# Running the whole gated embedding before the experts, and adding it to the stream in SBUF

## The chip, the cores and the metric

The kernel runs on one core of a Trainium2 chip. The metric is the device time of one execution in microseconds (us); lower is better. Three executions before the change gave a median of 1067.1 us.

## The reference, cut to what matters

The model has two layers (DEPTH = 2) on a stream h of 512 tokens by 1024 columns. Behind the mixers and the first layer norm, each layer adds a mixture of 16 experts and a gated per-layer embedding, both computed from the same h, and normalises the sum:

```python
    h = layer_norm(DN_ALPHA * h + mix, ln1_g[i], ln1_b[i])
    y_moe = hier_moe(h, moe_wgc[i], moe_bgc[i], moe_wgf[i], moe_bgf[i],
                     moe_w1[i], moe_w3[i], moe_w2[i])
    y_ple = jax.nn.sigmoid(h @ ple_wg[i] + ple_bg[i]) * (p[i] @ ple_wp[i])
    h = layer_norm(DN_ALPHA * h + y_moe + y_ple, ln2_g[i], ln2_b[i])
```

An expert is a gated MLP of width 256 on the tokens routed to it: silu(t @ w1) * (t @ w3), then @ w2, weighted by its gate. Each token goes to 2 of the 16. The embedding's product h @ ple_wg is 512 x 1024 x 1024.

## The kernel before, in words

**Products.** Weights and activations are float32. A chunk of weights is loaded raw, split into a high and a low part (`split`, lines 224 and 225: ScalarE casts the high part, VectorE subtracts to get the low one), and each product is three matmuls (`mm3`, lines 218 to 220).

**The planner.** `plan` lists all units of weight work of a layer in order; a unit is one chunk, mostly 512 KB. `pump` issues a unit's loads on SP's queue (line 240) `ahead_raw` units ahead of the one that TensorE works on, and its split `ahead_split` units ahead. `fill(n)` emits n units, `fill_us(us)` emits pieces of units worth so many planned us (a piece of an embedding unit is one of its four token tiles, 6 matmuls), `fill_to` all up to a mark. Engines run in order, each in its own queue; the compiler may move independent instructions past one another.

**Slots.** Raw chunks, high and low parts, the stream tiles `h`, transposed tokens `xT`, expert outputs `ye`, and the embedding's `pwp`, `bg` and `plz` all take one of 33 slots of 4 KB a partition (`NSLOT`). A slot is given again only when its last user is done, be it a matmul or a store. Half-size tiles have 6 slots of their own.

**The embedding before.** `add_pwp` computes p @ ple_wp for both column halves ahead of it. `add_ple(i, c)` is the gate's product for half c: four units of 24 matmuls, with the four token tiles in four PSUM banks. At the last unit `ple_tile` adds the bias (VectorE), takes tanh (ScalarE) and multiplies by `pwp` (VectorE); every two token tiles, a DMA of POOL's queue adds the result to the DRAM array `yd` (`accum_op=OP.add`, line 1228). `norm1` has stored h both to `hd`, from which the experts gather, and to `yd`. Half 0 runs between routing and the experts. Half 1 is cut in two parts (`PLE_AT = 3, 12`): two units after expert 3, whose sums are kept in `plz`, and two after expert 12.

**The experts.** `layer` routes the tokens (`route`), gathers the rows of two experts from `hd` by indirect DMAs, tests whether any expert has over 128 tokens (`overflow`: every engine loads the count into a register and branches, lines 1343 and 1344), then loops over 16 experts. An expert has four units for w1 and w3 (24 matmuls) and two for w2 (12 matmuls), the latter emitted while the next expert's are under way. Its gathered rows are transposed first (`expert_x`, line 376), its activations in between (`expert_act`, line 1292). The outputs of 14 experts are added to `yd` by a scattering DMA (`scatter`, line 1257); the last two are added on TensorE after the stream has been read back from `yd` (`load_stream`, line 1411; `tail_sum`, line 1430).

**Loads ahead.** `P_MOE = 14, 3` holds from routing to expert 10, `P_END = 7, 3` from there (`E_END`), `P_LAST = 8, 4` at the last expert.

Of the kernel before, what the change touches and what calls it, by code (L numbers as in the profile page):

```python
# [13 lines left out]
AF = mybir.ActivationFunctionType  # L14
OP = mybir.AluOpType
# [136 lines left out]
class Trunk:  # L152
# [14 lines left out]
    ]  # L167
    N = [[5.5, 2.0, 1.5, 2], [5.5, 0, 3.5, 3.5]]
    R = [[3.0, 9.0], [6.0, 7.0]]
    W6 = [[2, 4, 1.5], [2, 2, 0.5]]  # L170
    E_END = 10
    PLE_AT = 3, 12
    P_LAST = 8, 4
    P_END = 7, 3
    P_LN = 14, 1
    P_MOE = 14, 3
    APART = [[], [0, 1, 3]]
    ZPE = [[1], [1, 2, 3]]

# [821 lines left out]
    def norm1(self, i, t):  # L1001

        self.ln_tile(t, t in self.APART[0])
        h = self.h[t]
        for dst in (self.hd, self.yd):
            self.nc.gpsimd.dma_start(dst[t * 128:(t + 1) * 128], h)
        self.dump(f"h1_{i}_{t}", h)


# [190 lines left out]

        self.add([(lambda r: r, self.A["ple_wp"][i][:, cs].rearrange("(k p) n -> p k n", p=128))], [2, 512], emit)

    def ple_tile(self, t, c, z, bias, o):

        nc = self.nc
        nc.vector.tensor_add(o, z, bias)
        nc.scalar.activation(o, o, AF.Tanh, scale=0.5)
        nc.vector.scalar_tensor_tensor(o, o, 1.0, self.pwp[c][t // 2][:, t % 2], op0=OP.add, op1=OP.mult)

    def add_ple(self, i, c, part=None):  # L1210

        nc = self.nc
        cs = slice(c * 512, (c + 1) * 512)
        qs = range(4) if part is None else range(part * 2, part * 2 + 2)
        st = {}

        def evac(t, ps):
            if part == 0:
                if t % 2 == 0:
                    self.plz[t // 2] = self.s4([128, 2, 512], "plz")  # L1220
                nc.vector.tensor_add(self.plz[t // 2][:, t % 2], ps, self.bg[:, cs])
            else:
                if part is None and t % 2 == 0:
                    self.plz[t // 2] = self.s4([128, 2, 512], "plz")
                z = self.plz[t // 2]
                self.ple_tile(t, c, ps, z[:, t % 2] if part else self.bg[:, cs], z[:, t % 2])
                if t % 2:
                    nc.gpsimd.dma_start(self.yd[(t - 1) * 128:(t + 1) * 128, cs].rearrange("(t p) n -> p t n", p=128),
                                        z, accum_op=OP.add)

        def emit(q):
            def f(wp):
                if q == qs[0]:
                    st["ps"] = [self.ps("pl") for _ in range(NT)]
                for t in range(NT):
                    for k in range(2):
                        self.mm3(st["ps"][t], [x[:, q * 2 + k, t * 128:(t + 1) * 128] for x in self.hT],
                                 [x[:, k] for x in wp], q == qs[0] and k == 0, q == qs[-1] and k == 1)
                    if q == qs[-1]:
                        evac(t, st["ps"][t])  # L1240
                    yield 1.28
            return f

        for q in qs:
            src = self.A["ple_wg"][i][q * 256:(q + 1) * 256, cs].rearrange("(k p) n -> p k n", p=128)
            self.add([(lambda r: r, src)], [2, 512], emit(q))

# [207 lines left out]
    def plan(self, i):  # L1455

        m = self.marks = getattr(self, "marks", {})
        here = lambda name: m.__setitem__((i, name), len(self.units))
        self.add_head(i, 0, before=lambda t: self.start_norm(i, t))
        self.add_hyena(i, 2)  # L1460
        self.add_hyena(i, 1)
        self.add_hyena(i, 0)
        self.add_pool(i)
        here("pool")
        self.add_head(i, 1)
        here("head1")
        self.add_mix(i, (0, 1, 6, 7), 0, True)
        self.add_head(i, 2)
        here("head2")
        self.add_mix(i, (0, 1, 6, 7), 1, True)  # L1470
        self.add_head(i, 3)
        here("head3")
        for c in range(2):
            self.add_mix(i, (2, 3, 4), c, False)
        here("mix")
        self.add_last_mix(i)
        here("last")
        self.add_pwp(i, 0)
        self.add_pwp(i, 1)
        here("pwp")  # L1480
        self.add_ple(i, 0)
        here("ple")
        for e in range(NE):

            self.add_expert_in(i, e)
            if e > 0:
                self.add_expert_out(i, e - 1)
            if e in self.PLE_AT:
                self.add_ple(i, 1, self.PLE_AT.index(e))
        self.add_expert_out(i, NE - 1)  # L1490
        here("end")

# [16 lines left out]
    def layer(self, i):  # L1509
        nc, A = self.nc, self.A  # L1510
# [94 lines left out]
        next(r)  # L1605
        self.fill_us(self.R[i][0])
        for _ in r:
            pass
        self.xe, self.xT, self.act, self.actT, self.yl, self.hotT, self.plz = {}, {}, {}, {}, {}, {}, {}
        self.ahead_raw, self.ahead_split = self.P_MOE  # L1610
        for e in range(2):
            self.xe[e] = self.gather(self.rows[:, e:e + 1])
        self.fill_us(self.R[i][1])
        self.overflow(i)
        self.fill_to(i, "ple")
        self.expert_x(0)
        for e in range(NE):
            self.fill(2)
            if e + 2 < NE:
                self.xe[e + 2] = self.gather(self.rows[:, e + 2:e + 3])  # L1620
            if e == self.E_END:
                self.gb = self.gain(A["ln2_g"][i], A["ln2_b"][i])
                self.ahead_raw, self.ahead_split = self.P_END
            if e + 1 < NE:
                self.expert_x(e + 1)
            self.fill(2)
            if e == NE - 1:
                self.load_stream()
            if e >= NE - NL:
                self.last_places(e)  # L1630
            if e == NE - 1:
                self.ahead_raw, self.ahead_split = self.P_LAST

                self.cap = self.marks[i, "end"] + 3
            if e > 0:
                self.fill(2)
            self.expert_act(e)
            if e in self.PLE_AT:
                self.fill(2)
        self.fill(2)  # L1640

    def build(self):
# [56 lines left out]
```

## Time and profile before

| what | value |
|---|---|
| median of 3 runs (lowest, highest) | 1067.1 us (1065.82, 1071.48) |
| the profiled execution: its own time | 1060.65 us |
| its span, first to last instruction | 1058.7 us |
| mean granted TensorE clock | 0.974 of full speed |
| TensorE busy | 977.4 us, 92% |
| VectorE, ScalarE, POOL busy | 74%, 58%, 16% |
| SP's DMA queue (weights) | 155.58 MB, 44.8% of the 16 DMA engines' span |
| POOL's DMA queue (gathers, scatters, stores, tables) | 40.87 MB, 15.1% |

The profile is of one execution; its sums are set against 1060.65 us, of which the span is all but 1.95 us. Times within it are counted from the span's start. In layer 0 the embedding's half 0 runs from 307 to 336 us and the experts from 339 to 539 us; in layer 1 from 810 to 838 us and from 842 to 1034 us.

### The profile page before, as it was taken

Reading aid. Unit: us, or ns where it says so; the run is one execution under the profiler, and the core shown is the slowest. Engines: PE = TensorE matmul, PEld = TensorE weight load, DVE = VectorE, ACT = ScalarE, POOL = GpSimd, SP = SyncE. Lnnn points to the kernel's source line nnn. Section 1 sums busy time; section 2 is a strip of 40 time slices with the busy share of each in tenths; the row PEclk is TensorE's granted clock in tenths of the full one; section 3 lists DMA queues with packets and bytes.
Section 4 is the critical chain, followed back from the end, with each engine's and each line's share of the span. In section 5 each row is a group of like instructions: output and inputs, shape, how many; then the busy total and the mean of one; then the engine's idle time right before and its main releaser. Section 6 shows DMA issues by size and latency. Waiting matters only on the chain. (4 is left out here: it accounts for less than half of the span.)

```text
span 1058.7 us, 14409 instructions
## 1 busy us (share of the span) xinstructions
PE 977.4 (92%) x4869; PEld 805.7 (76%) x4870; DVE 779.3 (74%) x1301; ACT 613.5 (58%) x1046; POOL 166.3 (16%) x170
## 2 busy tenths in 40 slices
PE   4999999999889898999999999999998989999895
PEld 3887889897767676777768889798776768877673
DVE  7576887767685676878885578847678677888776
ACT  5425464656552746887754246654645375887673
POOL 1101000000122112332121100000002222333112
PEclk9999999999999998999989999999999999999998
DMA  8815121231864988999994412122186498899974
GB/s 261 234 35 140 51 79 42 70 95 65 308 209 109 334 245 274 292 300 308 264 312 122 112 55 66 49 64 88 50 307 221 107 329 275 283 311 318 306 211 159
DMA packets 156010, 197.49 MB, mean 187 GB/s; under 512 B 20296, under 2 KB 123786, under 8 KB 155925
## 3 DMA queue, kind: packets, MB, share of 16 engines
q1 hardware_dynamic: 135253, 155.58, 44.8%
q0 software_dynamic: 20672, 40.87, 15.1%
q8 instruction: 42, 0.69, 0.3%
q14 instruction: 43, 0.35, 0.1%
HBM read 182.85 MB, written 29.36 MB: 200 GB/s over the span
## 5 line engine op out<-in xcount | busy, mean ns | idle before, releaser
L225 DVE TENSOR_TENSOR wlo<-raw,whi 128x1024 fp32r<-128x1024 f32 (+2 forms) x278 | 321.9, 1182 | 78.9 <-ACT whi L224 68.1
L224 ACT CAST whi<-raw 128x1024 fp32r<-128x1024 f32 (+2 forms) x278 | 275.0, 1025 | 42.1 <-DMA yd<-ye,rt_tok 11.0
L218 PE MATMUL e<-whi,xT 128*128 128x512 f32 x256 | 108.8, 425 | 3.5 <-ACT xT L224 1.8
L219 PE MATMUL e<-wlo,xT 128*128 128x512 f32 x256 | 106.0, 414 | 5.9 <-DVE wlo L225 5.9
L220 PE MATMUL e<-whi,xT 128*128 128x512 f32 x256 | 103.4, 404 | 0.0
L218 PE MATMUL pj<-whi,hT 128*128 128x384 f32 x256 | 89.8, 351 | 2.3 <-ACT hT L224 1.8
L219 PE MATMUL pj<-wlo,hT 128*128 128x384 f32 x256 | 88.0, 344 | 0.3 <-DVE wlo L225 0.3
L220 PE MATMUL pj<-whi,hT 128*128 128x384 f32 x256 | 87.2, 341 | 0.2
L1257 POOL DMA_INDIRECT yd<-ye,rt_tok x28 | 47.0, 1677 | 196.5 <-ACT ye L1322 115.5
L868 ACT ACTIVATE prob<-sc,mx 128x512 f32<-128x512 f32 x64 | 43.7, 687 | 38.9 <-DVE mx L867 37.8
L219 PEld LDWEIGHTS e<-wlo,xT 128*128 128x128 f32 x256 | 50.0, 195 | 20.8 <-DVE wlo L225 12.0
L1251 POOL DMA_INDIRECT xe<-hd,rt_tok x32 | 48.2, 1507 | 100.4 <-PE tr L376 55.8
L218 PEld LDWEIGHTS e<-whi,xT 128*128 128x128 f32 x256 | 50.0, 195 | 14.5 <-ACT whi L224 3.5
L308 POOL TENSOR_TENSOR ors<-rs_y,mhalf 128x4 f32<-128x4 f32 x8 | 8.5, 1057 | 333.8 <-DVE rs_y L307 333.8
L220 PEld LDWEIGHTS e<-whi,xT 128*128 128x128 f32 x256 | 49.6, 194 | 10.2
L218 PE MATMUL mo<-whi,YT 128*128 128x512 f32 x128 | 53.6, 419 | 0.2 <-ACT YT L224 0.2
L219 PE MATMUL e<-wlo,actT 128*128 128x512 f32 x128 | 52.4, 409 | 1.2 <-DVE wlo L225 1.2
L218 PEld LDWEIGHTS pj<-whi,hT 128*128 128x128 f32 x256 | 48.7, 190 | 4.8 <-ACT hT L224 2.5
L218 PE MATMUL e<-whi,actT 128*128 128x512 f32 x128 | 48.5, 403 | 3.7 <-ACT whi L224 2.8
L219 PE MATMUL pl<-wlo,hT 128*128 128x512 f32 x128 | 51.3, 401 | 0.5 <-DVE wlo L225 0.5
L218 PE MATMUL pl<-whi,hT 128*128 128x512 f32 x128 | 51.1, 405 | 0.4 <-ACT whi L224 0.4
L220 PE MATMUL pl<-whi,hT 128*128 128x512 f32 x128 | 51.3, 401 | 0.0
(340 smaller groups left out, 2317.0 us busy)
## 6 DMA issues: line engine op xcount, KB each, us to landing
raw<-in_moe_w_dram SPq DMA_DIRECT2D x256, 256.0 KB
raw<-in_moe_w_dram SPq DMA_DIRECT2D x64, 512.0 KB
raw<-in_w_in_dram SPq DMA_DIRECT2D x96, 128.0 KB
raw<-in_w_in_dram SPq DMA_DIRECT2D x16, 512.0 KB
raw<-in_ple_wg_dram SPq DMA_DIRECT2D x16, 512.0 KB
raw<-in_w_out_dram SPq DMA_DIRECT2D x14, 512.0 KB
tabi<-c_tabi_dram POOLq DMA_DIRECT2D x8, 516.0 KB, 4.9
tabf<-c_tabf_dram POOLq DMA_DIRECT2D x8, 512.0 KB, 5.5
```

The source lines that it names most:

```text
L218: mm(ps, a[0], b[0], start=start, stop=False)
L219: mm(ps, a[0], b[1], start=False, stop=False)
L220: mm(ps, a[1], b[0], start=False, stop=stop)
L224: self.nc.scalar.copy(hi, src)
L225: self.nc.vector.tensor_sub(lo, src, hi.bitcast(F32))
L308: nc.gpsimd.tensor_tensor(out, y, self.mhalf[:, :n], op=OP.pow)
L868: nc.scalar.activation(p[:, c], o, AF.Exp, bias=mx[:, c:c + 1], accum_out=sm[:, c:c + 1])
L1251: self.nc.gpsimd.indirect_dma_start(out=x, out_offset=None, in_=self.hd[:, :], in_offset=bass.IndirectOffsetOnAxis(ap=tok, axis=0), bounds ...
L1257: self.nc.gpsimd.indirect_dma_start(out=self.yd[:, :], out_offset=bass.IndirectOffsetOnAxis(ap=row, axis=0), in_=y, in_offset=None, bounds ...
```

## The change

The two halves of the embedding both run, uncut, between routing and the experts. `ple_tile` adds its result to `h` in SBUF (VectorE) in place of the accumulating DMA to `yd`, and when a token tile has both halves, stores it to `yd` once; `norm1` stores to `hd` alone. The result `o` takes a half-size slot. `expert_x(0)` and `overflow` move: the transposes of expert 0 are emitted some 24 planned us into the embedding, the test for overflow after all of it. During the embedding 14 chunks are loaded ahead (`P_PLE`), from there 20 (`P_MOE`), from expert 10 on 12 (`P_END`, which was 7). `R` lists the planned us of embedding work between the steps of routing: before 3.0 and 9.0 (layer 1: 6.0 and 7.0), now 3.0, 1.0, 9.0, 14.0 (6.0, 1.0, 9.0, 14.0), the last three in a row.

```diff
-    R = [[3.0, 9.0], [6.0, 7.0]]
+    R = [[3.0, 1.0, 9.0, 14.0], [6.0, 1.0, 9.0, 14.0]]
-    PLE_AT = 3, 12
-    P_END = 7, 3
+    P_END = 12, 3
-    P_MOE = 14, 3
+    P_PLE = 14, 3
+    P_MOE = 20, 3
...
-        for dst in (self.hd, self.yd):
-            self.nc.gpsimd.dma_start(dst[t * 128:(t + 1) * 128], h)
+        self.nc.gpsimd.dma_start(self.hd[t * 128:(t + 1) * 128], h)
...
-    def ple_tile(self, t, c, z, bias, o):
+    def ple_tile(self, t, c, z):
         nc = self.nc
-        nc.vector.tensor_add(o, z, bias)
+        cs = slice(c * 512, (c + 1) * 512)
+        o = self.s2([128, 512], "plz")
+        nc.vector.tensor_add(o, z, self.bg[:, cs])
         nc.scalar.activation(o, o, AF.Tanh, scale=0.5)
         nc.vector.scalar_tensor_tensor(o, o, 1.0, self.pwp[c][t // 2][:, t % 2], op0=OP.add, op1=OP.mult)
+        h = self.h[t]
+        nc.vector.tensor_add(h[:, cs], h[:, cs], o)
+        if c == 1:
+            nc.gpsimd.dma_start(self.yd[t * 128:(t + 1) * 128], h)
...
-                if t % 2:
-                    nc.gpsimd.dma_start(self.yd[(t - 1) * 128:(t + 1) * 128, cs].rearrange("(t p) n -> p t n", p=128),
-                                        z, accum_op=OP.add)
...
         self.add_ple(i, 0)
+        self.add_ple(i, 1)
         here("ple")
...
-            if e in self.PLE_AT:
-                self.add_ple(i, 1, self.PLE_AT.index(e))
...
-        self.ahead_raw, self.ahead_split = self.P_MOE
+        self.ahead_raw, self.ahead_split = self.P_PLE
         for e in range(2):
             self.xe[e] = self.gather(self.rows[:, e:e + 1])
         self.fill_us(self.R[i][1])
-        self.overflow(i)
-        self.fill_to(i, "ple")
-        self.expert_x(0)
+        self.fill_us(self.R[i][2])
+        self.fill_us(self.R[i][3])
+        self.expert_x(0)
+        self.fill_to(i, "ple")
+        self.overflow(i)
+        self.ahead_raw, self.ahead_split = self.P_MOE
...
-            if e in self.PLE_AT:
-                self.fill(2)
```

## Rows read from the trace of the kernel before

**Rows 1.** The page: busy time, share and instructions of each engine.
```profile
PE 977.4 (92%) x4869; PEld 805.7 (76%) x4870; DVE 779.3 (74%) x1301; ACT 613.5 (58%) x1046; POOL 166.3 (16%) x170
```
**Rows 2.** Stretches: length, busy of PE, PEld, DVE, ACT, POOL; clock; DMA share; GB/s.
```profile
306.80:336.00 29.20, 29.20 (x146) 23.33 (x145) 18.18 (x56) 7.54 (x12) 2.13 (x2) 0.94 0.29 90
342.00:380.00 38.00, 33.04 (x145) 26.53 (x144) 27.91 (x32) 25.90 (x36) 9.63 (x7) 0.91 1.00 309
...
440.00:531.00 91.00, 87.13 (x398) 67.53 (x397) 75.89 (x88) 70.72 (x99) 24.03 (x15) 1.00 0.92 286
...
342.00:531.00 189.00, 175.48 (x788) 138.63 (x787) 146.40 (x168) 135.44 (x187) 46.20 (x30) 0.96 0.91 285
...
960.00:1022.00 62.00, 57.76 (x255) 44.35 (x253) 49.05 (x58) 45.23 (x63) 12.77 (x8) 0.97 0.99 311
844.50:1022.00 177.50, 169.55 (x772) 133.60 (x771) 141.87 (x164) 131.90 (x184) 45.50 (x29) 0.98 0.96 303
```
**Rows 3.** TensorE in order of time, layer 0: start, length, what, [idle before].
```profile
313.13 0.40 PE L218 MATMUL pl<-whi,hT 128*128 128x512 f32 x1
...
319.15 0.39 PE L220 MATMUL pl<-whi,hT 128*128 128x512 f32 x1
...
335.62 0.40 PE L220 MATMUL pl<-whi,hT 128*128 128x512 f32 x1
337.00 1.18 PE L376 MATMUL tr<-cst,xe 128*128 128x128 f32 x8 [0.99 <-DVE plz L1206]
339.10 0.51 PE L218 MATMUL e<-whi,xT 128*128 128x512 f32 x1 [0.92 <-ACT xT L224]
...
352.70 1.04 PE L376 MATMUL tr<-cst,xe 128*128 128x128 f32 x8
353.49 0.48 PE L218 MATMUL e<-whi,xT 128*128 128x512 f32 x1
...
417.19 0.69 PE L1292 MATMUL e<-cst,act 128*128 128x128 f32 x2 [4.68 <-DVE act L1275]
...
538.60 2.52 PE L1430 MATMUL el<-yl,hotT 128*128 128x512 f32 x4 [1.57 <-ACT yl L1315]
```
**Rows 4.** The same in layer 1.
```profile
838.30 0.40 PE L220 MATMUL pl<-whi,hT 128*128 128x512 f32 x1
...
841.72 0.51 PE L218 MATMUL e<-whi,xT 128*128 128x512 f32 x1 [0.86 <-ACT xT L224]
...
1033.83 3.34 PE L1430 MATMUL el<-yl,hotT 128*128 128x512 f32 x11
```
**Rows 5.** Groups of SP's loads: from 200 to 339 us, then from 342 to 531 us.
```profile
L240 SPq DMA_DIRECT2D raw<-in_moe_w_dram x28: 328/414/1303, 266.3 to 335.8; - x28
...
L240 SPq DMA_DIRECT2D raw<-in_moe_w_dram x132: 327/404/3282, 341.7 to 529.3; - x132
```
**Rows 6.** A stretch of layer 1 with two accumulating stores in flight (columns of Rows 2).
```profile
842.80:846.50 3.70, 3.70 (x20) 3.10 (x19) 3.68 (x5) 3.70 (x6) 3.09 (x3) 1.00 0.94 174
```
**Rows 7.** The embedding's VectorE and ScalarE work, and its DMA issues (KB, us to landing).
```profile
L1207 ACT ACTIVATE plz<-plz x16: 630/632/636, 332.6 to 1002.5; 128x512 f32<-128x512 f32 x16
L1208 DVE SCALAR_TENSOR_TENSOR plz<-plz,pwp x16: 681/686/694, 333.6 to 1003.1; 128x512 f32<-128x512 f32 x16
L1221 DVE TENSOR_TENSOR plz<-pl,bg x8: 685/689/692, 389.8 to 893.9; 128x512 f32<-128x512 f32 x8
...
yd<-h POOLq DMA_DIRECT2D x8, 512.0 KB, 5.2
yd<-plz POOLq DMA_DIRECT2D x8, 512.0 KB, 8.9
```
**Rows 8.** Who waited: TensorE, 280 to 560 us; SP, 440 to 531 us; ScalarE, 406 to 420 us.
```profile
PE e L1292 <- DVE act L1275: 9.6, 3, 4.7
...
SPq L240 <- DMA yd<-ye,rt_tok: 17.0, 3, 8.7
...
414.50 1.04 ACT L224 CAST whi<-raw 128x1024 fp32r<-128x1024 f32 x1 [5.72 <-issue]
```
**Rows 9.** SP's waits over the whole span, one of them; the first expert output's scatter.
```profile
SPq L1343 <- DVE rt_cnt L1131: 26.0, 2, 16.7
...
361.19 1.87 POOL L1257 DMA_INDIRECT yd<-ye,rt_tok  x1 [6.19 <-ACT actT L224]
```

More of the change, by code (lines that the diff above doesn't have):

```diff
@@ L1201, in add_pwp, with add_ple @@
         self.add([(lambda r: r, self.A["ple_wp"][i][:, cs].rearrange("(k p) n -> p k n", p=128))], [2, 512], emit)
-    def ple_tile(self, t, c, z, bias, o):
+    def ple_tile(self, t, c, z):
         nc = self.nc
-        nc.vector.tensor_add(o, z, bias)
+        cs = slice(c * 512, (c + 1) * 512)
+        o = self.s2([128, 512], "plz")
+        nc.vector.tensor_add(o, z, self.bg[:, cs])
         nc.scalar.activation(o, o, AF.Tanh, scale=0.5)
         nc.vector.scalar_tensor_tensor(o, o, 1.0, self.pwp[c][t // 2][:, t % 2], op0=OP.add, op1=OP.mult)
-    def add_ple(self, i, c, part=None):
-        nc = self.nc
+        h = self.h[t]
+        nc.vector.tensor_add(h[:, cs], h[:, cs], o)
+        if c == 1:
+            nc.gpsimd.dma_start(self.yd[t * 128:(t + 1) * 128], h)
+    def add_ple(self, i, c):
         cs = slice(c * 512, (c + 1) * 512)
-        qs = range(4) if part is None else range(part * 2, part * 2 + 2)
         st = {}
[L1217 to L1226, printed above, removed]
-                if t % 2:
-                    nc.gpsimd.dma_start(self.yd[(t - 1) * 128:(t + 1) * 128, cs].rearrange("(t p) n -> p t n", p=128),
-                                        z, accum_op=OP.add)
         def emit(q):
             def f(wp):
-                if q == qs[0]:
+                if q == 0:
                     st["ps"] = [self.ps("pl") for _ in range(NT)]
@@ L1237, in f @@
                         self.mm3(st["ps"][t], [x[:, q * 2 + k, t * 128:(t + 1) * 128] for x in self.hT],
-                                 [x[:, k] for x in wp], q == qs[0] and k == 0, q == qs[-1] and k == 1)
-                    if q == qs[-1]:
-                        evac(t, st["ps"][t])
+                                 [x[:, k] for x in wp], q == 0 and k == 0, q == 3 and k == 1)
+                    if q == 3:
+                        self.ple_tile(t, c, st["ps"][t])
                     yield 1.28
             return f
-        for q in qs:
+        for q in range(4):
             src = self.A["ple_wg"][i][q * 256:(q + 1) * 256, cs].rearrange("(k p) n -> p k n", p=128)
@@ L1608, in layer @@
             pass
-        self.xe, self.xT, self.act, self.actT, self.yl, self.hotT, self.plz = {}, {}, {}, {}, {}, {}, {}
-        self.ahead_raw, self.ahead_split = self.P_MOE
+        self.xe, self.xT, self.act, self.actT, self.yl, self.hotT = {}, {}, {}, {}, {}, {}
+        self.ahead_raw, self.ahead_split = self.P_PLE
         for e in range(2):
```

## The prediction

> **What bounds the kernel now.** I read the page's busy shares first, then a table of stretches, TensorE's order of time at the seams, SP's loads, and the waits. TensorE is busy 92% of the span [rows 1], so only a stage in which it loses time can give any. Two neighbouring stages differ. In the embedding block (306.8 to 336 us) TensorE has no gap to speak of and the DMA engines are at 0.29; among the experts the DMA share is 1.00 at first, 0.91 over 342 to 531 us and 0.96 over 844.5 to 1022 us [rows 2]. The expert stage is near both limits at once, and that is where the change works.
>
> TensorE's own need there: 27 embedding matmuls start between 313.13 and 319.15 us, so one takes 6.02 / 26 = 0.2315 us at full clock [rows 3]. An expert has 36 matmuls, 8 transposes of tokens, 0.79 us together (352.70 to 353.49), and 2 of activations, at the same 0.1 us each: 16 experts are 16 x (8.33 + 0.79 + 0.2) = 149 us. Half 1 of the embedding, 96 matmuls, adds 22.2 us. From the first expert matmul to the final sum's first (`el`) there are 199.5 us in layer 0 [rows 3] and 192.1 us in layer 1 [rows 4]. So 28.3 and 20.9 us are lost: to waits, and to a clock granted at 0.91 in layer 0's first stretch [rows 2] (2.4 GHz, in parts 1.2, behind idle gaps). The longest wait, 4.68 us at 417.19 [rows 3], is for an activation that stands behind a split on ScalarE, itself waiting 5.72 us [rows 8]; SP waits in the same manner for slots held by scatters, 17.0 us in three waits [rows 8]. Slots, then, pass a late scatter on to the loads and the splits.
>
> **The change, part by part.**
>
> *Half 1 goes ahead.* Per layer 22.2 us of TensorE leave the expert stage and stand before it: nothing gained, nothing lost on TensorE. Its four chunks leave too. At 311 GB/s and a share of 0.99 [rows 2], 0.524 MB take 1.67 us of all DMA engines, so 6.7 us of DMA go where it idles.
>
> *Accumulating stores vanish.* Four per layer, 0.524 MB each [rows 7]. With little but two of them in flight the engines were at 0.94 and moved 174 GB/s [rows 6], or 185 at a full share, so two cost 1.05 MB / 185 = 5.7 us. Half 1's pair lies inside the expert stage, and about half of half 0's pair. Bounds for these three stores: 5 us at the chunks' rate, 8.5 at the measured one; I take 8.5, since the row is of this very store. The single store to `yd` moves from before routing to the block's end, where DMA engines idle; nobody needs it until the first scatter, which now comes 22 us behind the first expert matmul [rows 3, 9]. Its four issues precede expert 2's gather on POOL's queue, which waits for the last VectorE add; the gather is needed an expert later.
>
> *VectorE.* Four adds per layer (`plz<-pl,bg` of the first part, 0.69 us) go, eight adds to `h` come. At about 0.69 us, from the same operand size [rows 7], that is 2.8 us more, in a block where VectorE has 11 of 29 us free. The block's last unit, though, needs 4 x 3 x 0.69 + 1.2 = 9.5 us of VectorE against 24 x 0.2315 = 5.6 of TensorE, so VectorE ends up to 3.9 us late, with the first expert's splits queued behind it. Those splits run up to three units ahead: between 0 and 3.9 us per layer, I take 1, since only the last of them can be caught.
>
> *Expert 0's transposes move into the block.* From the last embedding matmul to the first expert one there are 3.48 us [rows 3], 3.42 in layer 1 [rows 4]. The transposes' 0.79 and 1.4 us up to 337.00 (branch and PSUM) stay as they are, paid in the block or behind it; about 1.3 us per layer go.
>
> *The overflow test moves behind the block.* SP waited 26.0 us at it, twice in all, for the routing's count [rows 9]; behind the block the count is long there. Worth nothing by itself: 28 loads (12 pairs and 4 singles, 16 chunks) were issued by 335.8 us [rows 5], ahead of need. Every engine still pays its branch once.
>
> *Deeper loads.* With 20 instead of 14 (and 12 instead of 7) units ahead, DMA need not stop when TensorE stalls. Slots limit it: at the block's end 11 raw, 8 split, 4 `h`, 4 `pwp`, `bg` and 2 `xT` take 30 of 33. So between 0 and 6 extra chunks are in by the first expert; I take 2, 3.3 us of DMA. Among the experts 17 raw, 8 split, 4 `xT` and a `ye` are 30 as well, against 29 now (11 raw, and 5 for `plz`, `pwp` and `bg`), so late scatters should stall splits as often as now.
>
> **The sum, by the DMA engines.** Busy now: 0.91 x 189 = 172.0 us and 0.96 x 177.5 = 170.4 us. Less 6.7 and 8.5: 156.8 and 155.2. With loads always waiting I take a share of 0.98, between the 0.92 of 440 to 531 us and the 1.00 and 0.99 of the best stretches [rows 2], and near those as the change removes the cap that made the low ones: 160.0 and 158.4, less 3.3: 156.7 and 155.1. Around the stretch lie 2.9 us before and 7.6 behind in layer 0; in layer 1 2.8 before and 11.8 behind, of which I take 9.7, the middle between the layers. The expert stage becomes 167.2 and 167.6 us. What it has now without half 1 is 199.5 - 22.2 = 177.3 and 192.1 - 22.2 = 169.9. Gains 10.1 and 2.3; with 2.6 at the seams and 2 lost to VectorE: 13.0 us. The profiled execution would go from 1060.65 to 1047.7 us. It stands 6.4 us under the median of the runs shown, so I take the same 13.0 from 1067.1: **1054.1 us**.
>
> **Rivals.**
>
> *TensorE is the bound, and waits halve.* If the deeper buffer takes away half of the 28.3 and 20.9 us, the stages are 163.2 and 159.5 us, gains 14.1 and 10.4, with the seams 25 us: 1042. For it: SP's waits for scatters [rows 8], which a deeper buffer could bridge. Against it: the DMA sum above is longer than this.
>
> *The stage only shifts.* The waits stay, because they come from the order of instructions on ScalarE and VectorE and from slots, which are as scarce as before, or the 20 are never reached. The longest group, 9.6 us in three waits for `act` [rows 8], has its longest in the first half, at 417 us [rows 3], with 16 chunks in at the start [rows 5]; that speaks for this. Then only 0.6 us at the seams: 1066.5.
>
> *DMA idles longer than it saves: slower.* The block is now 51 us in which TensorE is full and DMA is not, and the experts have no product left that needs few loads. If the share stays at 0.91 and 0.96 (splits and SP still stuck behind scatters' slots) and the stores cost half of what I took, the stretches are (172.0 - 10.9) / 0.91 = 177.0 and (170.4 - 10.9) / 0.96 = 166.1 us, the stages 187.5 and 180.7: 10.2 and 10.8 us longer than the room left. Less two chunks per layer and the seams: 14 slower, 1081. It decides if the DMA share among the experts stays under some 0.93. The Trainium skill, Perfetto Trace Analysis, section "Optimization Strategy", says that where the most contended engine changes from regime to regime, interleaving the regimes may help; this change takes two interleaved ones apart. By that rule the outcome is this rival's; the trace agrees as far as there are two regimes, DMA at 0.29 and at 0.91 to 1.00 [rows 2].
>
> **How the numbers follow.** The forecast has 0.40, the halved waits 0.16, the mere shift 0.23, the slower case 0.21. Half a per cent, 5.3 us, is about what a measurement of this kernel can tell from no change. Faster by more: the first two, 0.56; within it: the shift, 0.23; slower: 0.21. The range 1041 to 1077 holds the forecast with its bounds (no head start of chunks 1060.7, stores at the chunks' rate and VectorE's full lag 1067; six chunks of head start 1041), the shift and most of the second rival; left out are most of the slower case and a little below.
>
> **What would show it.** Right: DMA share of 0.97 or more from the first expert to the last; the expert stages some 32 and 25 us shorter and the block some 21 longer; no accumulating stores of `plz`; the first expert matmul about 2.2 us behind the last embedding one; fewer waits of SP for `yd<-ye`. Wrong: a DMA share that stays at 0.91, raw chunks as the releaser of splits through the second half of each layer, or a gap at the block's end where splits wait behind VectorE's adds.

## The result, and the profile after

The change makes the kernel slower: a median of 1094.07 us (four runs, 1089.91 to 1094.78) beside 1067.5 us for the kernel before (four runs), a ratio of 1.0263 with a 95% interval of 1.022 to 1.0307. The forecast was 1054.1 us, its range 1041 to 1077. The profiled execution of the changed kernel has a span of 1092.6 us against 1058.7, so 33.9 us are to be found. By the medians it is 26.6: the profiled execution of before took 1060.65 us, 6.9 under its median.

Lines of the page of the changed kernel: busy shares, the two DMA queues (packets, MB, share of 16 engines), the chain that ended last, and three groups with the idle time before them and what ended it.

```profile
PE 991.1 (91%) x4869; PEld 815.4 (75%) x4870; DVE 784.5 (72%) x1309; ACT 613.6 (56%) x1046; POOL 152.4 (14%) x162
q1 hardware_dynamic: 135253, 155.58, 43.5%
q0 software_dynamic: 18496, 36.67, 12.0%
DMA yd<-ye,rt_tok 15%; PE pj L220 3%; PE pj L218 3%; PE pj L219 3%; PE e L219 2%; DMA xe<-hd,rt_tok 2%; PE e L220 2%; PE e L218 2%; DVE wlo L225 1%; ACT whi L224 1%; PE mo L218 1%; PE mo L220 1%; PE mo L219 1%; DMA raw<-in_w_in_dram 1%; PE tr L376 1%
L225 DVE TENSOR_TENSOR wlo<-raw,whi 128x1024 fp32r<-128x1024 f32 (+2 forms) x278 | 321.1, 1183 | 102.4 <-ACT whi L224 89.7
L224 ACT CAST whi<-raw 128x1024 fp32r<-128x1024 f32 (+2 forms) x278 | 273.9, 1025 | 67.0 <-DMA yd<-ye,rt_tok 29.6
L218 PE MATMUL e<-whi,xT 128*128 128x512 f32 x256 | 114.1, 446 | 27.5 <-ACT whi L224 12.1
```

The stores did go: POOL's DMA queue falls from 40.87 MB and 15.1% to 36.67 MB and 12.0%. But of the 67.0 us that ScalarE idles before its splits, 29.6 are put down to the scatters of expert outputs (`yd<-ye`), where the page of before has 11.0. These scatters, which [rows 8] showed holding SP, take 15% of the span in the chain that ended last.

TensorE in order of time in the changed kernel, answering [rows 3, 4]: where the embedding ends and the experts begin in each layer, and where each final sum begins:

```profile
307.24 0.40 PE L218 MATMUL pl<-whi,hT 128*128 128x512 f32 x1
...
357.44 0.40 PE L220 MATMUL pl<-whi,hT 128*128 128x512 f32 x1
366.95 0.79 PE L218 MATMUL e<-whi,xT 128*128 128x512 f32 x1 [9.11 <-ACTq L1334]
...
559.67 1.01 PE L1420 MATMUL el<-yl,hotT 128*128 128x512 f32 x3
...
833.97 0.39 PE L218 MATMUL pl<-whi,hT 128*128 128x512 f32 x1
...
884.42 0.39 PE L220 MATMUL pl<-whi,hT 128*128 128x512 f32 x1
891.08 0.79 PE L218 MATMUL e<-whi,xT 128*128 128x512 f32 x1 [6.28 <-DVE wlo L225]
...
1067.60 0.40 PE L1420 MATMUL el<-yl,hotT 128*128 128x512 f32 x1
```

From such rows come the lengths used from here on. The *seam* of a layer runs from the start of the last embedding matmul to that of the first expert matmul, the *stage* from there to the first `el`. In layer 1 of the kernel before, the first `el` stands at 1032.53 us, one short matmul ahead of the group shown in [rows 4]. The numbers of before are without half 1's 22.2 us.

| us | before | after | more |
|---|---|---|---|
| seam, layer 0 | 3.5 | 9.5 | 6.0 |
| expert stage, layer 0 | 177.3 | 192.7 | 15.4 |
| its end to layer 1's embedding | 272.6 | 274.3 | 1.7 |
| seam, layer 1 | 3.4 | 6.7 | 3.2 |
| expert stage, layer 1 | 168.6 | 176.5 | 7.9 |

The embedding blocks and what lies before the first and behind layer 1's stage make up the rest, -0.3 us. So 32.5 of 33.9 us are in the two stages the change was to shorten, and at their seams.

Stretches of the changed kernel (columns of [rows 2]):

```profile
307.00:336.00 29.00, 28.91 (x152) 23.65 (x153) 21.13 (x60) 10.18 (x15) 2.13 (x2) 1.00 0.33 104
366.00:376.00 10.00, 9.05 (x31) 7.34 (x32) 3.21 (x4) 4.30 (x6) 1.04 (x1) 0.65 0.74 275
368.00:560.00 192.00, 169.27 (x729) 130.92 (x727) 138.85 (x158) 135.36 (x188) 43.21 (x31) 0.92 0.87 274
891.00:1067.00 176.00, 163.88 (x722) 127.58 (x723) 136.74 (x157) 132.25 (x184) 46.13 (x31) 0.94 0.88 282
```

The DMA share among the experts fell, from 0.91 and 0.96 [rows 2] to 0.87 and 0.88. DMA is not what became short: 0.87 x 192 is 167 us of DMA work, where the kernel before had 0.91 x 189 = 172. The clock shows the idle time too: behind a seam of 9.5 us TensorE is granted 0.65 for the next 10 us, and 0.92 over the stage.

The waits in layer 0's stage of the changed kernel, in one view per engine (what waits, for what: us in total, times, longest):

```profile
PE e L218 <- ACT whi L224: 11.2, 8, 2.5
PE e L218 <- ACTq L1334: 9.1, 1, 9.1
PE e L219 <- DVE wlo L225: 8.7, 9, 4.4
...
ACT whi L224 <- DMA yd<-ye,rt_tok: 19.5, 7, 4.1
ACT L224 <- DMA yd<-h: 5.6, 1, 5.6
...
SPq L240 <- DMA yd<-ye,rt_tok: 10.1, 3, 6.0
```

TensorE waits for splits, and none of ScalarE's waits in this view is for a raw chunk. What it waits for is the *place* of its output: a slot whose last user, a scatter or the store of h, has not landed. In the same stage of the kernel before the views have such waits of ScalarE too, but small, and larger ones of SP (339 to 538.6 us):

```profile
ACT whi L224 <- DMA yd<-plz: 3.6, 2, 2.2
ACT whi L224 <- DMA yd<-ye,rt_tok: 1.8, 2, 1.5
...
SPq L240 <- DMA yd<-ye,rt_tok: 22.5, 5, 8.7
```

The 5.72 us of [rows 8], put down to nothing there, may be one more of ScalarE's: with slots of their own for `ye` (below) the kernel before has no such wait.

In layer 1 these waits did not grow. First the changed kernel (890 to 1071 us), then the kernel before (842 to 1034 us):

```profile
ACT whi L224 <- DMA yd<-ye,rt_tok: 10.1, 2, 5.3
...
ACT whi L224 <- DMA yd<-ye,rt_tok: 9.2, 2, 5.6
```

So their growth can be behind layer 0's 15.4 us, and not behind layer 1's 7.9.

### The profile page after: what moved, and what is told of

Same layout as the page of the kernel before. It is cut to its first block, busy times and chain, and to the rows that moved or that the text cites. A ratio compares the mean times of both kernels' runs of the same rounds, so it can differ in the third digit from the quotient of the medians.

```text
span 1092.6 us, 14414 instructions
## 1 busy us (share of the span) xinstructions
PE 991.1 (91%) x4869; PEld 815.4 (75%) x4870; DVE 784.5 (72%) x1309; ACT 613.6 (56%) x1046; POOL 152.4 (14%) x162
## 3 DMA queue, kind: packets, MB, share of 16 engines
q0 software_dynamic: 18496, 36.67, 12.0%
## 4 chain that ended last, share of the span: by engine, by line
PE 27%; DMA 18%; issue 12%; ACT 3%; DVE 3%; POOL 1%; POOLq 0%; SPq 0%; DVEq 0%; ACTq 0%
DMA yd<-ye,rt_tok 15%; PE pj L220 3%; PE pj L218 3%; PE pj L219 3%; PE e L219 2%; DMA xe<-hd,rt_tok 2%; PE e L220 2%; PE e L218 2%; DVE wlo L225 1%; ACT whi L224 1%; PE mo L218 1%; PE mo L220 1%; PE mo L219 1%; DMA raw<-in_w_in_dram 1%; PE tr L376 1%
## 5 line engine op out<-in xcount | busy, mean ns | idle before, releaser
L224 ACT CAST whi<-raw 128x1024 fp32r<-128x1024 f32 (+2 forms) x278 | 273.9, 1025 | 67.0 <-DMA yd<-ye,rt_tok 29.6
L218 PE MATMUL e<-whi,xT 128*128 128x512 f32 x256 | 114.1, 446 | 27.5 <-ACT whi L224 12.1
L219 PE MATMUL e<-wlo,xT 128*128 128x512 f32 x256 | 112.0, 437 | 4.9 <-DVE wlo L225 4.7
L220 PE MATMUL e<-whi,xT 128*128 128x512 f32 x256 | 107.6, 420 | 0.0
L218 PEld LDWEIGHTS e<-whi,xT 128*128 128x128 f32 x256 | 52.7, 206 | 40.7 <-ACTq L1334 16.2
L219 PEld LDWEIGHTS e<-wlo,xT 128*128 128x128 f32 x256 | 52.9, 207 | 21.8 <-DVE wlo L225 11.9
L1241 POOL DMA_INDIRECT xe<-hd,rt_tok x32 | 44.8, 1401 | 143.5 <-PE tr L376 97.5
L225 DVE TENSOR_TENSOR xT<-tr,xT 128x512 fp32r<-128x512 f32 x64 | 41.1, 685 | 27.7 <-ACT xT L224 27.6
L220 PEld LDWEIGHTS e<-whi,xT 128*128 128x128 f32 x256 | 52.4, 205 | 10.8
L224 ACT CAST xT<-tr 128x512 fp32r<-128x512 f32 x64 | 34.8, 600 | 31.6 <-PE tr L376 31.5
L218 PE MATMUL pj<-hT,whi 128*128 128x512 f32 x128 | 51.4, 403 | 0.0
L219 PE MATMUL pj<-hT,whi 128*128 128x512 f32 x128 | 51.2, 400 | 0.0
```

The lines of the kernel that those rows point to most:

```text
L218: mm(ps, a[0], b[0], start=start, stop=False)
L219: mm(ps, a[0], b[1], start=False, stop=False)
L220: mm(ps, a[1], b[0], start=False, stop=stop)
L224: self.nc.scalar.copy(hi, src)
L225: self.nc.vector.tensor_sub(lo, src, hi.bitcast(F32))
L1241: self.nc.gpsimd.indirect_dma_start(out=x, out_offset=None, in_=self.hd[:, :], in_offset=bass.IndirectOffsetOnAxis(ap=tok, axis=0), bounds ...
```

## The experiments

Eighteen kernels ran, each beside the kernel before on the same chip (medians of before 1061.3 to 1063.5 us). Ratios are to it. Where nothing else is said a kernel is the changed one with the edit shown.

### Which part costs: the restructured embedding, or the depth of the loads

The changed embedding with the loads ahead of before:

```diff
-    P_END = 12, 3
+    P_END = 7, 3
-    P_MOE = 20, 3
+    P_MOE = 14, 3
```

> The changed kernel with loads ahead as before (14 among the experts, 7 near the end). Theory A, slots: with 20 chunks ahead, splits and expert outputs are left with slots whose scatter or store has not landed; then this run wins back most of the 15 us that layer 0's expert stage lost: 1068 to 1078 us. Theory B, the seam: the time is lost where the block ends (overflow test, stores of h, VectorE's adds), 9.5 and 6.7 us without a matmul; then this run stays within 5 us of the changed kernel's 1094. Theory C, regimes: the experts need the embedding's matmuls between them; then 1090 or more too.

1068.64 us, ratio 1.0085 (1.0048 to 1.0122). The reverse, the kernel before with the deeper loads alone:

```diff
-    P_END = 7, 3
+    P_END = 12, 3
-    P_MOE = 14, 3
+    P_MOE = 20, 3
```

> The kernel before with 20 chunks ahead among the experts and 12 near the end, nothing else. Theory A: slower by 5 to 25 us, more than in the changed kernel as plz, pwp and bg still hold five slots; splits wait for scatters more often. Theories B and C: no difference over 5 us.

1109.78 us, ratio 1.0453 (1.0414 to 1.0492). The depth costs some 47 us in the kernel before, where half 1's `plz`, `pwp` and `bg` still hold slots, nearly twice what was expected at most. In the changed kernel it costs 25.4 us by the medians (1094.07 less 1068.64) and 19 by the ratios (1.0263 less 1.0085): the kernel before took 1067.5 us beside the one and 1062.4 beside the other, and differences to 1094.07 below have this uncertainty of some 5 us. The traces put the cost in the seams, in layer 0's stage (192.7 us against 175.4) and in the hand-over behind it (274.3 against 270.1). Layer 1's stage is no longer with the deep loads, 176.5 us against 178.2. In layer 0's stage of these two kernels, first the shallow changed kernel's stretch, which has a DMA share of 0.94:

```profile
362.00:537.00 175.00, 160.77 (x726) 123.36 (x727) 138.09 (x158) 134.47 (x186) 47.24 (x32) 0.98 0.94 302
```

and then the deep kernel of before, 0.83, with SP's wait:

```profile
346.00:565.00 219.00, 190.22 (x809) 147.23 (x809) 151.61 (x172) 141.69 (x192) 45.58 (x30) 0.92 0.83 254
...
SPq L240 <- DMA yd<-ye,rt_tok: 32.6, 6, 10.0
```

More loads asked for, fewer in flight. Of the 17 us between the first of these stretches and the changed kernel's 368 to 560 us, TensorE is idle for 8.5 and busy for 8.5 longer on as many matmuls, at a clock of 0.92 against 0.98. In the kernel before with deep loads ScalarE's splits wait for no scatter in this stage (its transposed tokens do, 9.6 us), so how much of the 47 us is the scatters' slots is not shown.

### The rest of the restructured embedding

Half 1 ahead of the experts in the kernel before, and nothing else (accumulating stores, the test for overflow ahead of the block, 14 and 7):

```diff
         self.add_ple(i, 0)
+        self.add_ple(i, 1)
...
-            if e in self.PLE_AT:
-                self.add_ple(i, 1, self.PLE_AT.index(e))
```

> The kernel before with half 1 whole ahead of the experts, but with its accumulating stores, loads 14 and 7, and the overflow test where it was. Theory C: as slow as the changed kernel, 1085 or more. Theories A and B: within 8 us of 1067.

1066.68 us, 1.003 (0.9997 to 1.0064): no change of the total that can be told. Its seams are 2 us shorter each, layer 0's stage is 176.7 us against 177.3, and layer 1's 173.6 against 168.6. To this the moves of expert 0's transposes and of the test were added:

```diff
-        self.overflow(i)
-        self.fill_to(i, "ple")
+        self.fill_us(14.0)
         self.expert_x(0)
+        self.fill_to(i, "ple")
+        self.overflow(i)
```

> The run before this one, with expert 0's transposes inside the block and the overflow test behind it, as in the change. Theory B: 6 to 12 us slower than the run before this one, with over 5 us without a matmul at the block's end. Theories A and C: within 4 us of it.

1070.75 us, 1.0096 (1.0061 to 1.0131). From here to the shallow changed kernel (1.0085) little but the accumulation is left, DMA against VectorE: nothing by the total. So the restructuring costs some 0.9%, most of it, by the medians, when the moves were added. The shallow kernel again, with its additions to `h` on POOL:

```diff
-        nc.vector.tensor_add(h[:, cs], h[:, cs], o)
+        nc.gpsimd.tensor_add(h[:, cs], h[:, cs], o)
```

> The changed kernel with loads 14 and 7, and the eight adds to h of each layer on POOL's engine in place of VectorE's. Theory B: the gap at the block's end (5.0 and 4.1 us) comes from VectorE's queue, so it falls to 2.8 to 3.5 and the time by 2 to 4 us, to about 1065. If the gap comes from the branch, or POOL's adds hold up the stores or VectorE, it stays or grows.

1068.58 us, 1.0101 (1.0051 to 1.0152): the seams fall from 5.0 and 4.1 to 3.0 and 2.5 us, and the time stays, as layer 0's stage grows from 175.4 to 181.2.

The seam of layer 0 can now be read as a ladder: half 1 ahead alone, then with the test behind the block, then the shallow changed kernel. One row of TensorE's order from each:

```profile
359.37 0.50 PE L218 MATMUL e<-whi,xT 128*128 128x512 f32 x1 [0.24 <-ACT xT L224]
```

```profile
360.07 0.51 PE L218 MATMUL e<-whi,xT 128*128 128x512 f32 x1 [2.43 <-ACTq L1344]
```

```profile
362.22 0.79 PE L218 MATMUL e<-whi,xT 128*128 128x512 f32 x1 [4.57 <-ACTq L1334]
```

The seams are 1.5, 2.8, 5.0 us, and 9.5 with 20 units: the moves cost 1.3 although they take the transposes out of the seam, the additions on VectorE about 2, the deeper loads 4.5. `ACTq L1334` is ScalarE's branch at that test.

### Which of the two depths, and from what moment

12 near the end kept, 14 before it; then 17 and 12:

```diff
-    P_MOE = 20, 3
+    P_MOE = 14, 3
```

> The changed kernel with 14 chunks ahead among the experts and the 12 near the end kept. Theory A, slots: from expert 10 on 12 ahead leave some eight slots free, so the 12 do no harm and the 20 cost it all: 1063 to 1072 us, as the run with 14 and 7. If the 12 are half of the harm: 1078 or more.

```diff
-    P_MOE = 20, 3
+    P_MOE = 17, 3
```

> The changed kernel with 17 ahead in place of 20. Theory A: the harm sets in when the free slots run out (17 raw of 20, 8 split, 4 xT and a ye are 30 of 33; with 17 it is 27), so 1063 to 1076 us. A loss in proportion to the depth would give about 1081.

1077.45 us (1.017, 1.0126 to 1.0213) and 1073.75 us (1.0129, 1.0086 to 1.0172). So 12 near the end, which the slots' theory took to be harmless, costs 8.8 us beside 7 at a depth of 14 (1068.64), and 17 is no dearer than 14. Then 20 kept, and 7 near the end:

```diff
-    P_END = 12, 3
+    P_END = 7, 3
```

> The changed kernel with P_END back to 7 and P_MOE left at 20 from the block's end. Theory A (the 20 units are what holds the splits, from the seam on): layer 0's expert stage stays near 192 us and its seam near 9.5 us, since both lie ahead of expert 10, and the time is about 1085 us. Theory B (the 12 units near the end are the dearer part): layer 0's stage falls towards 180 us and the time to about 1078 us.

1085.3 us, 1.0225 (1.0183 to 1.0268), with seams of 9.4 and 6.6 and stages of 190.8 and 174.4 us. So 20 instead of 14 costs 16.7 us (1068.64 to 1085.3). What 12 instead of 7 adds at that depth is less sure: 8.8 us by the medians (to 1094.07), 4 by the ratios, whose intervals overlap.

Where the 12 cost is plain at a depth of 14: in the hand-over to layer 1, 282.3 us there from the first `el` to layer 1's embedding, 270.1 with 7. VectorE in order of time in the kernel with 14 and 12, and what TensorE waited for:

```profile
543.81 0.08 DVE L1426 DVE_READ_ACCUMULATOR h<-h,el 128x1 f32 x1
546.96 1.23 DVE L225 TENSOR_TENSOR wlo<-raw,whi 128x1024 fp32r<-128x1024 f32 x1 [3.08 <-ACT whi L224]
548.49 1.22 DVE L225 TENSOR_TENSOR wlo<-raw,whi 128x1024 fp32r<-128x1024 f32 x1 [0.30 <-ACT whi L224]
549.99 1.23 DVE L225 TENSOR_TENSOR wlo<-raw,whi 128x1024 fp32r<-128x1024 f32 x1 [0.28 <-ACT whi L224]
551.13 0.68 DVE L1426 SCALAR_TENSOR_TENSOR h<-h,el 128x512 f32<-128x512 f32 x1
...
PE tr L376 <- DVE h L350: 9.5, 1, 9.5
```

With 14 and 7 the second row of `h<-h,el` stands directly behind the first:

```profile
543.11 0.08 DVE L1426 DVE_READ_ACCUMULATOR h<-h,el 128x1 f32 x1
543.11 0.68 DVE L1426 SCALAR_TENSOR_TENSOR h<-h,el 128x512 f32<-128x512 f32 x1
...
PE tr L376 <- DVE h L350: 1.3, 1, 1.3
```

Three splits for the next layer's first product stand in VectorE's queue ahead of the layer norm on which that layer waits. In the changed kernel this wait is 3.1 us, and what the 12 cost there is not in one place: against the kernel with 20 and 7, each stage and the hand-over are some 2 us longer.

The other question is the moment: the 20 set one expert later, when h's stores have landed.

```diff
-        self.ahead_raw, self.ahead_split = self.P_MOE
         for e in range(NE):
+            if e == 1:
+                self.ahead_raw, self.ahead_split = self.P_MOE
```

> The changed kernel, but the 20 ahead are set only from expert 1 on; expert 0 keeps 14. If the seam's extra 4.5 and 2.6 us (over the run with 14 and 7) come from raw chunks that take the slots of the splits there, which are then left with those of h whose store is under way, the gap falls to about 5 and 4 us, and the time by some 7 us, to 1087. If the gap comes from the overflow test and VectorE's adds alone, it stays at 9.5 and 6.7.

1079.05 us, 1.0138 (1.0107 to 1.017): 15 us less than the changed kernel by the medians, 13 by the ratios. The seams are those of 14 units again, 5.0 and 4.1 us, but layer 0's stage is still 187.2 us, and ScalarE waits 16.4 us there for `yd<-ye`, in seven waits. With 7 near the end as well:

> 20 units from expert 1 on and 7 near the end, with ye still in the shared slots: differs from the kernel that has ye in hT's memory (1064.1 us) by ye's place alone. If scatters' slots are what makes deep loads dear, the time is 8 us or more above that, about 1072, with waits of ScalarE for yd<-ye of 10 us and more in layer 0; if the moment of the switch and P_END explain it all, it is 1064 to 1067 us, with such waits under 5 us.

1073.53 us, 1.0111 (1.0069 to 1.0153), stages 185.6 and 173.6; ScalarE still waits 14.8 us for `yd<-ye` in layer 0.

### Whose slots they are

First, two of the 33 slots set aside for `ye`, 31 left for the rest, with 20 and 12 and then with 20 and 7:

```diff
-    NSLOT = 33
+    NSLOT = 31
...
-                    y = self.s4([128, 1024], "ye")
+                    y = self.slots.tile([128, 1024], F32, name="ye", tag="ye", bufs=2)
```

> The changed kernel, 20 and 12 ahead, with two slots of their own for the experts' outputs ye and 31 for all else: no split or load can be given a slot whose scatter is still under way. Theory A1, it is the scatters in the slots: most of layer 0's loss comes back, 1068 to 1080 us, and ScalarE's 19.5 us of waits for scatters in that stage fall under 5. Theory A2, it is bare scarcity, whoever held the slot: no better than 1088, as the others have fewer slots still.

> The changed kernel with two slots of their own for ye (31 for all else), 20 ahead among the experts and 7 near the end. If the 12 near the end cost their 10 us at the hand-over to layer 1 (there, VectorE's splits of the next layer's weights stand ahead of the layer norm), this run loses that wait and comes to 1073 to 1079 us, against 1085.9 with 12. If the hand-over's wait comes from the 31 slots, it stays at 1083 or more.

1085.89 us (1.0237, 1.0194 to 1.0281) and 1076.95 us (1.0136, 1.0102 to 1.0169). With 7 near the end that is 8.4 us less than with shared slots; with 12 the total misses the 1068 to 1080 us expected, and its 8.2 us less are 3 by the ratios, which are not apart. No slot was added, and the stages fall from 192.7 and 176.5 to 173.1 and 168.7, and from 190.8 and 174.4 to 169.6 and 168.1. The two slots are missed elsewhere: the seams grow to 12.1 and 8.8, and 11.8 and 11.3 us, and with 20 and 12 layer 0's embedding starts 6.1 us later and the hand-over takes 283.7 us instead of 274.3.

The same two slots for the kernel before, and for half 1 ahead alone with 17 and 7:

> The kernel before with two slots of their own for ye and 31 for all else, nothing more. Theory A1 holds for it too: the 5 us stall behind a scatter at 412 us goes, 1054 to 1062 us where before has 1062 on this chip; if the two slots fewer cost more than that, slower by 2 to 10 us.

> The kernel before with half 1 whole ahead of the experts, its accumulating stores kept, two slots of their own for ye (31 for all else), 17 ahead and 7 near the end. If scatter-held slots and late raw chunks were what the experts still waited for, the stages fall from 176.7 and 173.6 us to some 171 and 169, and the time to 1052 to 1060, ahead of the kernel before. If the interleaved embedding hid waits that nothing else can, or the 31 slots cost at the seam, it stays at 1064 or more.

1062.04 us (0.9992, 0.9964 to 1.002) and 1073.68 us (1.0087, 1.0062 to 1.0112): no gain in the total where the loads are shallow, and a small loss where 17 units came with it, where a gain was expected. The kernel before does get shorter stages by it (193.0 and 186.2 us instead of 199.5 and 190.8, half 1 included) and loses them at the hand-over, 281.3 us instead of 272.6.

Then `ye` at no cost in slots. With the whole embedding ahead, the memory of the stream's transposed parts `hT` is idle among the experts, and `ye` can lie there, so all 33 slots are left for the rest; 20 from expert 1, 7 near the end:

```diff
-                    y = self.s4([128, 1024], "ye")
+                    j = e // 2 % 4 * 2
+                    y = flat(self.yb[e % 2][:, j:j + 2])
...
+            if e == 0:
+                self.yb = [self.big.tile([128, 8, 512], F32, name=f"yb{x}", tag="big") for x in range(2)]
```

> The changed kernel with the experts' outputs ye in the memory of hT (free among the experts now that the embedding is done; eight places, 33 slots for all else), 20 ahead from expert 1 on, 7 near the end. If slots cost everything but the seam, the expert stages are 168 to 171 us, the seams about 5 and 4 us, the hand-over as before, and the time 1050 to 1062 us: faster than the kernel before by up to 1%. If half 1 among the experts hid something else, 1066 or more.

1064.11 us, 1.0014 (0.9987 to 1.004), not the 1050 to 1062 us expected. Stages 173.8 and 169.0 us; the waits for `yd<-ye` are gone from ScalarE, and of DMAs it is the raw chunks that it now waits for. Layer 0 of this kernel, the stretch and ScalarE's wait:

```profile
362.00:537.00 175.00, 161.43 (x724) 123.12 (x724) 140.45 (x160) 134.13 (x186) 49.33 (x33) 0.98 0.95 304
...
ACT whi L224 <- DMA raw<-in_moe_w_dram: 11.2, 12, 3.3
```

With 20 set at the block's end, as the change has it:

> ye in hT's memory, 7 near the end, but 20 units set at the block's end as in the changed kernel: differs from the kernel of 1064.1 us by the moment of the switch alone. If the four slots of h, still held by their stores, are what the early switch hands to the splits, both seams grow to 7 to 10 us and the time is 1071 us or more; if it was ye all along, the seams stay at 5 and 4 us and the time at 1064 us.

1065.59 us, 1.0036 (1.001 to 1.0062). Two rows of this kernel:

```profile
365.31 0.80 PE L218 MATMUL e<-whi,xT 128*128 128x512 f32 x1 [9.01 <-ACTq L1335]
...
ACT L224 <- DMA yd<-h: 5.5, 1, 5.5
```

Its seams are the long ones, 9.4 and 6.8 us: these are h's slots, not the scatters'. The total does not show them, as its stages are the shortest of all with 33 slots, 172.2 and 167.2. With 14 units in place of 20, and with half 1 ahead alone in place of the whole change:

> The run before this one with 14 ahead in place of 20. If without slots in the way depth serves, as I forecast, this one is slower than it by 4 to 12 us, with splits waiting for raw chunks. If depth is worth nothing, the two are within 3 us.

> The kernel before with half 1 whole ahead of the experts, accumulating stores kept, the overflow test where it was, ye in the memory of hT, 20 ahead from expert 1 on and 7 near the end. Seams of 1.5 us and stages of 168 to 172 us: 1046 to 1058 us, and 4 to 8 us ahead of the run with the adds in SBUF. If the accumulating stores hold back the experts, it is no faster than that one.

1067.37 us (1.0053, 1.0026 to 1.0079) and 1069.99 us (1.0062, 1.003 to 1.0093). With `ye` out of the way, then, 20 units are worth 3.3 us against 14. The last kernel, with the accumulating stores and the test ahead of the block, was expected at 1046 to 1058 us and 4 to 8 us ahead of the one with the additions in SBUF; it is 5.9 us behind it. Its seams are 1.5 us, but its stages are 178.1 and 174.2, where the other has 173.8 and 169.0.

Four of these kernels vary two things one at a time, at 20 and 7 (medians in us):

| | 20 from the seam | 20 from expert 1 |
|---|---|---|
| `ye` in the shared slots | 1085.3 | 1073.5 |
| `ye` in `hT`'s memory | 1065.6 | 1064.1 |

The place of `ye` is worth 19.7 and 9.4 us, the moment of the switch 11.8 and 1.5, the last within the noise. Either alone helps; most of the loss needs deep loads *and* slots that scatters hold. That `ye` in `hT` also frees a slot or two for the rest is not what does it, by the kernels with 31 slots. A test for overflow ahead of the block together with the additions in SBUF was not tried: its code adds to `yd`, which is stored only at the block's end.

## Why the prediction was wrong

**The step that failed** is "so late scatters should stall splits as often as now", under *Deeper loads*. It counted slots, 30 against 29 of 33, and took equal numbers for equal waits. In the changed kernel 19.5 us of ScalarE's time in layer 0 went to such waits; in the kernel before it was 1.8 (over the whole execution 29.6 and 11.0). The scatters were no slower, 8.6 us from issue to landing (median) and 8.8 before. What changed is who waits for them: SP's waits for `yd<-ye` did fall, as forecast, from 22.5 to 10.1 us in that stage, and ScalarE's grew. A reading that fits, though no trace shows the order in which slots are given: with more chunks asked for ahead, a slot is wanted sooner behind its last user, and the one that a scatter still holds falls to a split, which TensorE needs within three units, and no longer to a load, which it needs much later. The depth, a gain of 3.3 us per layer in the sum, cost 19 to 25 us. That it was slots and not DMA is shown by moving `ye` alone: 19.7 us.

**The sum by the DMA engines** had the work about right and the share wrong, and this step failed as well: with shallow loads, too, the change is 0.85% slower and not faster. In that kernel the 16 engines are busy for 166 and 162 us of the two stages, where the kernel before has 182 and 175: 17 and 14 us less, and the sum took off 15.2. But no kernel's share over a stage reached 0.98; they lie between 0.82 and 0.96. The sum gave stages of 167.2 and 167.6 us, gains of 10.1 and 2.3, the second from a stage read 1.3 us too long. Nearest to them is `ye` in `hT` with 20 from the seam, 172.2 and 167.2, gains of 5.1 and 1.4, and by another way. The share there is 0.91 over layer 0's stretch; but 38 loads, not 28 [rows 5], were issued by the first expert matmul, so six chunks more were on their way (ten loads are an expert's six chunks), where the sum took two. SP's loads from 200 us to that matmul, and the stretch behind it:

```profile
L240 SPq DMA_DIRECT2D raw<-in_moe_w_dram x38: 341/438/1036, 272.0 to 364.2; - x38
...
366.00:538.00 172.00, 163.45 (x730) 126.66 (x728) 139.27 (x158) 134.79 (x187) 51.97 (x31) 0.95 0.91 292
```

The changed kernel had its 38 loads out by 365.8 us as well, and could not use them: their splits had no place.

**The seams** had the wrong sign: -1.3 us each forecast, +6.0 and +3.2 measured. Half 1 ahead alone has a seam of 1.5 us with the transposes in it; with them gone from it and the test in it, it is 2.8. The row of that kernel has TensorE waiting 2.43 us for ScalarE's branch, so the test behind the block, "worth nothing by itself", costs at least 1.3 us. VectorE's lag, taken as 1 of up to 3.9 us, is about 2 by the additions on POOL. The largest term, 4.5 us, was not in the sum: h's four slots wait for the single store to `yd` at the block's end, and 20 units make the next splits take them. ScalarE and VectorE in the changed kernel (first the last addition to `h` and the next low part on VectorE, then ScalarE's splits and its next instruction):

```profile
362.19 0.69 DVE L1211 TENSOR_TENSOR h<-h,plz 128x512 f32<-128x512 f32 x1
...
367.63 1.23 DVE L225 TENSOR_TENSOR wlo<-raw,whi 128x1024 fp32r<-128x1024 f32 x1 [2.43 <-DMA yd<-h]
...
362.90 1.04 ACT L224 CAST whi<-raw 128x1024 fp32r<-128x1024 f32 x1 [1.46 <-DMA yd<-h]
365.23 1.04 ACT L224 CAST whi<-raw 128x1024 fp32r<-128x1024 f32 x1 [1.29 <-DVE wlo L225]
371.86 1.28 ACT L224 ACT_TABLE_LOAD   x1 [5.58 <-DMA yd<-h]
```

The prediction said of this store that "nobody needs it until the first scatter". Its data, no; its source's memory, at once. In the total it does not show by itself: with `ye` in `hT`, 20 from the seam and 20 from expert 1 cannot be told apart (1065.59 and 1064.11 us).

**The accumulating stores** went, as said, and some 29 us of the DMA engines' time with them (15.1% of 1058.7 us less 12.0% of 1092.6). With shallow loads and shared slots that is worth nothing by the total that the runs can tell (1.0096 with them, 1.0085 without). With `ye` in `hT` and 20 from expert 1, the kernel without them is 5.9 us ahead; since the test and the transposes differ there too, the stores' share of it is not shown. The row that priced these stores, [rows 6], held more than them: two gathers were issued in it, and weight loads have 0.14 of its share of 0.94.

**The rivals.** *The stage only shifts* is, by the total, what half 1 ahead does alone: 1.003. *TensorE is the bound, and waits halve* never came up. *Slower* had the sign and its own test, a DMA share under some 0.93, came true at 0.87; its price, 14 us, was about half, as it kept the old share where the share fell. It ascribed the loss to the two regimes being pulled apart, with splits and SP stuck behind scatters' slots as before and not more. The Trainium skill, Perfetto Trace Analysis, section "Optimization Strategy", says that interleaving regimes may help; by half 1 ahead alone, which takes them apart and changes nothing else, the rule is worth 0.3% here, with an interval that touches none. The Trainium skill, Perfetto Trace Analysis, section "Optimization Strategy", also says that the same gap repeating on the engine that should be full can mean that there is no room in memory for the next tile. The trace agrees: TensorE's waits for splits in layer 0 of the changed kernel come eight and nine times, 19.9 us in all; with `ye` in `hT` and 20 from the seam they are 5.4 us.

**Open.** Why layer 1's stage is 7.9 us longer: it is not the depth, as it is 178.2 us with shallow loads, where ScalarE waits 17.7 us for raw chunks, and 173.6 with half 1 ahead alone. What `P_END` costs in the changed kernel, and where. And why moving the test and the transposes costs 0.7% (1.003 to 1.0096) where the seams take 1.3 us each; the rest is in the stages, 181.1 and 176.2 against 176.7 and 173.6. No kernel tried beats the one before: the best, 1062.04 and 1064.11 us, are equal to it.

## What to carry to other kernels

When loads share memory with tiles that leave by DMA, the depth of the loads cannot be judged by counting slots: look at who holds the next slot to be given, and when its DMA lands. A wait for the place of an output looks like an engine waiting for a store that nobody reads; find it in the waits of the engine that makes the tile. Give tiles that leave by a slow DMA memory of their own before deepening the loads, and change the two depths, the moment and the place one at a time: here each hid the others.

## What the runs showed of the hardware

A store or a scatter keeps its source's memory far longer than its issue takes. The four stores of h in layer 0 were issued in 0.5 to 0.6 us each, and landed 4.8 to 8.6 us after that began (median 6.5) beside the loads of 20 units; beside those of 14 units it was 3.0 to 6.1 (median 4.7). In layer 1 the medians are 6.7 and 5.0. With 14 units only SP waited for these stores, 7.6 us over both layers. The scatters of `ye` were issued in 1.6 to 2.6 us, and landed after 8.6 us (median of 28) with 20 units and 8.5 with 14: they took no longer beside the deeper loads.

A seam is paid twice: over 366 to 376 us the clock was granted at 0.65 behind 9.1 us of idle TensorE, and the first expert's first dozen matmuls start 0.43 us apart instead of 0.23.
